# Last down projection of a hybrid encoder with its 512 tokens moved to the partitions: x turned by VectorE and transfers, final norm and output by groups of 128 tokens

## The chip, the cores and the metric

One core of a Trainium2 chip runs the whole program. The metric is the time of one execution on the device in microseconds (us); lower is better. TensorE (PE, with its weight loads PEld), VectorE (DVE), ScalarE (ACT), GpSimd (POOL) and the transfers (DMA, issued mostly by SyncE, SP) run beside each other, each engine its own instructions in order.

## The reference

Two layers on 512 tokens of width 1024 in float32. Each layer adds half a SwiGLU block, a mixer of attention and convolution, half a second SwiGLU block, and ends in an RMS norm:

```python
def swiglu(x, w_gate, w_up, w_down):
    return (jax.nn.silu(x @ w_gate) * (x @ w_up)) @ w_down
...
        x = x + 0.5 * swiglu(rms_norm(x, ffn2_norm[l]), ffn2_w_gate[l], ffn2_w_up[l], ffn2_w_down[l])
        x = rms_norm(x, post_norm[l])
    return x
```

`D_FF` is 2816. The change concerns the last `x @ w_down` of the second layer, the residual addition to it, and the last `rms_norm`.

## The kernel before

**Layout.** The residual `x` stays in on-chip memory as `[128, 8, 512]`: the 1024 features lie on the partitions in 8 blocks of 128, the 512 tokens along the free dimension. Every float32 product is made of three passes (`mm3`, lines 154 to 157): each operand is split into a high part (a cast on ScalarE, `hi`, `wh`) and a low part (a subtraction on VectorE, `lo`, `wl`), and high x high, high x low and low x high are added up in a bank of the accumulator memory. A weight tile of 128x1024 so costs one transfer, one cast of ScalarE (L240 or L144) and one subtraction of VectorE (L242 or L150).

**A SwiGLU block** (`ffn_body`) runs in units of up to four feature blocks of the 2816 (`UNITS = 2, 4, 4, 4, 4, 4`). The gate and up projections of a unit are made by a seven-product scheme on 2x2 blocks (`unit`), with sums of weight tiles made by VectorE (L338). The products are called by the operand that they use, in this order: `b11`, `b21`, `t2`, `t3`, `t1`, `t4`, `b22`, 24 matmuls each. They share banks: `t2` is added onto `bx`, `copied(bx)` (L354, on ScalarE) takes it away, and then `t1` is added onto the same two banks `bx`; `t3` and `t4` do the same on `bz`. So the first matmul of `t1` may only start when ScalarE has copied that bank.

The gated result of a unit has tokens on partitions and is turned for the down projection: VectorE transposes 32x32 blocks (L378), four transfers write a block to memory (`d<-e`, L384), two read it back as `r<-d` (L390), and `halved` (L396 on ScalarE, L397 on VectorE) splits it. A unit makes two such round trips through memory. Each unit's down projection is done while the next unit runs (`between`), so x is updated step by step (L486).

**The last stage** of a block takes the units that are left, the last two (8 feature blocks). Weights are stationary, activations `[128 features, 512 tokens]` are moved: for each of 8 output blocks, 8 x 3 matmuls of 128x512, then `update` adds the bank to `x[:, m, :]`, and `done(m)` does what the norm needs. In the last layer `done3` squares the block (ScalarE), adds it to a running sum (VectorE), and for the last block sums over the partitions by matmuls with a vector of ones (L193). Matmuls on ones (`idle`) fill TensorE's time there. After that comes `rsqrt` (a power on GpSimd, L173), `spread` (a diagonal matrix on VectorE, L207, and a matmul, L211, that puts the factor of each token into every partition), and eight products with gain and factor (L1018), each sent out as it is made (L1019).

**What sets the order.** The program is written in order, but a scheduler with its own estimate of durations decides how each engine's instructions stand; buffers come from pools that rotate: 4 each for `wh` and `wl`, 3 for `raw`, 9 for `fr` (the weight tiles of a unit), 7 banks called `ps`. A weight cast into `wh` waits until TensorE is through with the tile that lay in that buffer four tiles ago.

## Time and profile before

| | us |
|---|---|
| median of 3 runs | 1781.08 (1781.05 to 1782.27) |
| profiled execution, its own time | 1783.14 |
| its span | 1781.4 |
| TensorE's last matmul of the last stage starts | 1766.26 |
| mean granted TensorE clock | 0.996 |

| part of the span, us | VectorE busy | ScalarE busy | DMA share |
|---|---|---|---|
| 1680 to 1700 | 19.77 | 11.65 | 0.33 |
| 1720 to 1740 | 8.92 | 5.90 | 0.70 |
| 1740 to 1760 | 11.40 | 7.11 | 0.09 |

TensorE is busy for the whole of each of these stretches. In a timeline row, the first number is the start in us from the span's start, the second the time in us, then engine, line, operation, output and inputs, and in brackets how long the engine was idle before and for whom. A row with x2 or x8 merges instructions that follow each other.

### The profile page before, as it was taken

To read this page: it belongs to the slowest core of one execution; us is meant where nothing else is said; L and a number is where in the kernel's file an instruction comes from. 1 tells how busy PE (TensorE), PEld (TensorE's weight loads), DVE (VectorE), ACT (ScalarE), POOL (GpSimd) and SP (SyncE) were. 2 spreads that over 40 slices of the span, in tenths; PEclk is the share of its full clock that TensorE was granted. 3 is DMA by queue.
4 is the path that set the end of the run, shared out by engine and by line. 5 is a ranking of instruction groups with operands and counts; after the bars stand their busy time and mean duration, and the time that the engine had idled before them with its cause. 6 is when DMAs were issued, how large, how long until landed. Compare 5 with 4: busy or idle time off the path is not lost.

```text
span 1781.4 us, 22306 instructions
## 1 busy us (share of the span) xinstructions
PE 1756.3 (99%) x8208; PEld 1455.2 (82%) x8208; DVE 1403.5 (79%) x1984; ACT 946.4 (53%) x1472; POOL 277.7 (16%) x216
## 2 busy tenths in 40 slices
PE   8999999999999999999999999999999999999997
PEld 7788888888788888888888888888978788888886
DVE  7967877679869877878698778866979698678764
ACT  6544445457955544446555344444779455344442
POOL 4000000048842000000000000000688400000000
PEclk9999999999999999999999999999999999999999
DMA  8454434424225455343925344343250444345251
GB/s 287 138 165 143 146 110 126 135 77 130 49 104 133 128 158 164 109 152 94 290 78 170 114 154 142 113 125 115 80 152 3 159 115 163 131 142 161 88 154 60
DMA packets 119181, 234.09 MB, mean 131 GB/s; under 512 B 10272, under 2 KB 55712, under 8 KB 119072
## 3 DMA queue, kind: packets, MB, share of 16 engines
q1 hardware_dynamic: 115184, 219.72, 38.1%
q0 software_dynamic: 3456, 12.58, 3.9%
q8 instruction: 64, 1.05, 0.2%
q10 hardware_dynamic: 432, 0.38, 0.1%
q14 instruction: 45, 0.37, 0.1%
HBM read 207.47 MB, written 25.17 MB: 131 GB/s over the span
## 4 chain that ended last, share of the span: by engine, by line
PE 86%; DVE 4%; ACT 3%; DMA 3%; POOL 2%; issue 1%; SPq 1%; DVEq 0%; POOLq 0%; ACTq 0%
PE ps L157 27%; PE ps L155 27%; PE ps L156 27%; PE ps L796 2%; PE ps L762 1%; DVE wl L242 1%; DMA fr<-in_wgu 1%; DMA d<-e 1%; PE ps L783 1%; ACT pr L841 1%; PE ps L193 1%; POOL y L845 1%; ACT r L768 0%; DVE fr L338 0%; POOL sck L173 0%
## 5 line engine op out<-in xcount | busy, mean ns | idle before, releaser
L156 PE MATMUL ps<-wl,r 128*128 128x512 f32 (+2 forms) x1392 | 532.6, 384 | 1.6 <-DVE wl L242 1.4
L157 PE MATMUL ps<-wh,r 128*128 128x512 f32 (+2 forms) x1392 | 529.0, 384 | 2.7 <-DVE r L268 2.7
L155 PE MATMUL ps<-wh,r 128*128 128x512 f32 (+2 forms) x1392 | 514.2, 385 | 2.0 <-ACT wh L406 1.2
L240 ACT CAST wh<-fr 128x1024 fp32r<-128x1024 f32 x255 | 267.2, 1050 | 243.7 <-PE ps L156 113.4
L157 PE MATMUL ps<-r,wl 128*128 128x512 f32 x1008 | 391.0, 390 | 0.7 <-POOL wl L150 0.5
L156 PE MATMUL ps<-r,wh 128*128 128x512 f32 x1008 | 391.6, 390 | 0.0
L155 PE MATMUL ps<-r,wh 128*128 128x512 f32 x1008 | 386.8, 393 | 1.1 <-ACT r L396 0.7
L242 DVE TENSOR_TENSOR wl<-fr,wh 128x1024 fp32r<-128x1024 f32 x255 | 311.3, 1224 | 50.1 <-ACT wh L240 49.5
L157 PEld LDWEIGHTS ps<-wh,r 128*128 128x128 f32 x1392 | 261.8, 188 | 53.6 <-DVE r L268 3.6
L156 PEld LDWEIGHTS ps<-wl,r 128*128 128x128 f32 x1392 | 261.8, 188 | 53.3 <-DVE wl L242 3.3
L155 PEld LDWEIGHTS ps<-wh,r 128*128 128x128 f32 x1392 | 261.5, 188 | 53.1 <-ACT wh L406 1.4
L144 ACT CAST wh<-raw 128x1024 fp32r<-128x1024 f32 (+2 forms) x150 | 149.2, 1000 | 217.4 <-PE ps L156 95.0
L155 PEld LDWEIGHTS ps<-r,wh 128*128 128x128 f32 x1008 | 189.1, 188 | 43.6 <-ACT r L396 1.6
L157 PEld LDWEIGHTS ps<-r,wl 128*128 128x128 f32 x1008 | 189.3, 188 | 41.0 <-POOL wl L150 1.3
L156 PEld LDWEIGHTS ps<-r,wh 128*128 128x128 f32 x1008 | 189.3, 188 | 41.0 <-issue 1.4
L150 DVE TENSOR_TENSOR wl<-raw,wh 128x1024 fp32r<-128x1024 f32 (+3 forms) x134 | 157.2, 1175 | 70.5 <-ACT wh L144 69.2
L845 POOL TENSOR_TENSOR y<-y,pr 128x511 f32<-128x511 f32 (+14 forms) x120 | 157.9, 1316 | 56.3 <-ACT pr L841 49.5
L338 DVE TENSOR_TENSOR fr<-fr,fr 128x1024 f32<-128x1024 f32 x112 | 135.9, 1214 | 10.4 <-DMA fr<-in_wgu 10.4
L486 DVE TENSOR_TENSOR x<-ps,x 128x512 f32<-128x512 f32 x128 | 87.0, 685 | 71.9 <-PE ps L157 71.3
L173 POOL TENSOR_TENSOR rtok<-vtok,minus_half 128x4 f32<-128x4 f32 x8 | 10.4, 1303 | 743.6 <-DVE vtok L199 743.6
L368 ACT ACTIVATE e<-e,rtok 128x256 f32<-128x256 f32 x120 | 60.0, 508 | 83.9 <-DVE e L359 83.4
L397 DVE TENSOR_TENSOR r<-r,r 128x512 fp32r<-128x512 f32 x88 | 58.0, 679 | 56.2 <-ACT r L396 56.0
(175 smaller groups left out, 1732.1 us busy)
## 6 DMA issues: line engine op xcount, KB each, us to landing
fr<-in_wgu SPq DMA_DIRECT2D x175, 512.0 KB, 4.1
raw<-in_wd SPq DMA_DIRECT2D x64, 512.0 KB, 4.4
d<-e SPq DMA_DIRECT2D x176, 128.0 KB, 3.0
r<-d SPq DMA_DIRECT2D x88, 256.0 KB, 3.6
raw<-in_wd SPq DMA_DIRECT2D x32, 384.0 KB, 4.4
raw<-in_wcv SPq DMA_DIRECT2D x16, 512.0 KB, 3.2
raw<-in_wout SPq DMA_DIRECT2D x16, 512.0 KB, 3.7
raw<-in_wgu SPq DMA_DIRECT2D x8, 512.0 KB, 4.6
```

Of the source, the lines that this page charges most:

```text
L144: A.copy(hi[:, :w], raw[:, :w])
L150: (G if kind in POOLW.split() else V).tensor_tensor(lo[:, :w], raw[:, :w], hi[:, :w].bitcast(FP), ALU.subtract)
L155: T.matmul(o, lh, rh, start=first, stop=False, skip_group_check=free)
L156: T.matmul(o, lh, rl, start=False, stop=False, skip_group_check=free)
L157: T.matmul(o, ll, rh, start=False, stop=last, skip_group_check=free)
L240: order["cast"] = A.copy(hi[:, :w], src[:, :w]).ins
L242: V.tensor_tensor(lo[:, :w], src[:, :w], hi[:, :w].bitcast(FP), ALU.subtract)
L338: V.tensor_tensor(oh, ah, bh, ALU.add)
L368: A.activation(out[j][:, :h], src[j][:, :h], AF.Silu, scale=r)
L397: V.tensor_tensor(d, d.bitcast(FP), hi.bitcast(FP), ALU.subtract)
L486: V.tensor_tensor(xm, pd.rearrange("p (a t j) -> p t a j", a=4, t=NT), xm, ALU.add)
L845: order["conv"] = G.tensor_tensor(acc[:, s:], acc[:, s:], pr[:, s:], ALU.add).ins
```

## The change

In the last SwiGLU block of the last layer (`done is None`) the last stage is replaced by `end`:

- **x is turned.** VectorE transposes x in 32 instructions of 128x128 (four tiles `tb`, one for each block of 128 tokens, L521), and 16 transfers of 128 KB (32 partitions x 4 x 256 numbers, L528) put the pieces back into the memory of `x`, which then holds, as `xt`, 4 groups of 128 tokens on the partitions with 1024 features each. Both can be done as soon as the unit before has updated x, so they stand in the last unit.
- **The products are turned.** Activations are stationary (128 tokens of a feature block), weights `wend` `[128, 1024]` are moved in halves of 512: 8 accumulators (7 banks `ps` and one called `cv`), 4 groups x 2 halves. The first four feature blocks go through all accumulators; the last four finish one accumulator after the other. The weight tiles have the same size and number as before.
- **The norm goes by groups.** For each half: addition to `xt`, square with a sum along the free dimension on ScalarE. For each group: two small steps on VectorE, the power on GpSimd for one column, then one half of the output by VectorE and one by ScalarE, and two transfers of 256 KB. The post norm's gain is loaded once as `[128, 1024]` (`gend`) and is multiplied into the first half ahead of the factor.
- The host reorders the weights and the output for the block order that 32x32 transposes give.

```diff
+        ending = done is None
...
+        def weights(i):
+            raw = wpool.tile([P, WC], FP, tag="raw", name=nm("raw"), bufs=3)
+            nc.sync.dma_start(out=raw, in_=wend[i])
+            if i < 6:
+                return split_into("q", raw)
+            hi, lo = (fpool.tile([P, WC], FR, tag="fr", name=nm("fr"), bufs=FRB) for _ in range(2))
+            A.copy(hi, raw)
+            V.tensor_tensor(lo, raw, hi.bitcast(FP), ALU.subtract)
+            return hi, lo
+
+        def end(acts, ds):
+
+            n = len(ds)
+            tb = [fresh() for _ in range(NT)]
+            for m in range(KD):
+                for t in range(NT):
+                    V.transpose(tb[t].rearrange("p (a m j) -> p a m j", a=4, m=KD)[:, :, m],
+                                x[:, m, t * P:(t + 1) * P])
+            gb = fresh()
+            nc.sync.dma_start(out=gb, in_=gend)
+            xt = x.rearrange("p (a h) s -> p a (h s)", a=4)
+            for t in range(NT):
+                for b in range(4):
+                    nc.sync.dma_start(
+                        out=xt[t * 32:(t + 1) * 32, :, b * HS:(b + 1) * HS],
+                        in_=tb[t][b * 32:(b + 1) * 32].rearrange("p (a f) -> p a f", a=4))
+            os = [[bank() for _ in range(2)] for _ in range(3)]
+            os.append([bank(), psum.tile([P, S], FP, tag="cv", name=nm("cv"), bufs=1)])
...
+            for i in range(n):
+                w = weights(i)
+                for a in range(4):
+                    for h in range(2):
+                        part(os[a][h], acts[i], w, a, h, i == 0, False)
+            acts.extend(halved(d) for d in ds)
+            ws = [weights(i) for i in range(n, 2 * n)]
+            ss, ve = tiny("ssend", 8), tiny("veend", 4)
+            for a in range(4):
+                for h in range(2):
+                    f = slice(h * S, (h + 1) * S)
+                    for i in range(n):
+                        part(os[a][h], acts[n + i], ws[i], a, h, False, i == n - 1)
+                    V.tensor_tensor(xt[:, a, f], xt[:, a, f], os[a][h], ALU.add)
+                    A.activation(tmp(), xt[:, a, f], AF.Square, accum_out=ss[:, 2 * a + h:2 * a + h + 1])
+                    if h == 0:
+                        V.tensor_scalar(ve[:, a:a + 1], ss[:, 2 * a:2 * a + 1], 1.0 / D, EPS, ALU.mult, ALU.add)
+                        V.tensor_tensor(xt[:, a, f], xt[:, a, f], gb[:, f], ALU.mult)
+                V.scalar_tensor_tensor(ve[:, a:a + 1], ss[:, 2 * a + 1:2 * a + 2], 1.0 / D, ve[:, a:a + 1],
+                                       ALU.mult, ALU.add)
+                r = tiny("rend", 1)
+                rsqrt(r, ve[:, a:a + 1])
+                o = [slot(), slot()]
+                V.scalar_tensor_tensor(o[1], xt[:, a, S:WC], r, gb[:, S:WC], ALU.mult, ALU.mult)
+                nc.sync.dma_start(out=out[a, :, S:WC], in_=o[1])
+                A.activation(o[0], xt[:, a, 0:S], AF.Copy, scale=r)
+                (A if a == 3 else nc.sync).dma_start(out=out[a, :, 0:S], in_=o[0])
...
+        if ending:
+            return end(acts, ds)
...
-            ffn(l, ops, norm2, wgu2, wd2, done3)
-            r = tiny("rlast", NT)
-            rsqrt(r, ve)
-            ps = spread(r)
-            for m in range(KD):
-                o = slot()
-                V.scalar_tensor_tensor(o, x[:, m, :], gp[:, m:m + 1], ps, ALU.mult, ALU.mult)
-                nc.sync.dma_start(out=out[m], in_=o)
+            ffn(l, ops, norm2, wgu2, wd2, None)
```

Up to the last unit of this block the order of the instructions stays what it was, but for line numbers (one more from L320 on). In the last unit the scheduler places things anew. Three places follow; the number behind a name tells one buffer from the next, and the two programs number them apart by one.

**VectorE, start of the last unit**, before: `e_14217` is a gate result on its way to the first round trip, `e_14361` the block that this round trip will carry, `wl_14521` and `wl_14525` the low parts of the first weight tiles.

```order
L359 TENSOR_TENSOR e_14217<-ps_14254,e_14217 128x512
L242 TENSOR_TENSOR wl_14521<-fr_14499,wh_14519 128x1024
L359 TENSOR_TENSOR e_14217<-ps_14255,e_14217 128x512
L369 SCALAR_TENSOR_TENSOR e_14217<-e_14217,rh_12685 128x256
L338 TENSOR_TENSOR fr_14499<-fr_14499,fr_14507 128x1024
L242 TENSOR_TENSOR wl_14525<-fr_14501,wh_14523 128x1024
L378 STREAM_TRANSPOSE e_14361<-e_14217 128x8x32
```

The same place now:

```order
L360 TENSOR_TENSOR e_14216<-ps_14253,e_14216 128x512
L521 STREAM_TRANSPOSE fr_14826<-x 128x4x32 x8
L242 TENSOR_TENSOR wl_14520<-fr_14498,wh_14518 128x1024
L360 TENSOR_TENSOR e_14216<-ps_14254,e_14216 128x512
L370 SCALAR_TENSOR_TENSOR e_14216<-e_14216,rh_12684 128x256
L242 TENSOR_TENSOR wl_14524<-fr_14500,wh_14522 128x1024
L339 TENSOR_TENSOR fr_14498<-fr_14498,fr_14506 128x1024
L379 STREAM_TRANSPOSE e_14360<-e_14216 128x8x32
```

The first eight transposes of x stand ahead of the first weight tile's low part and of all that follows. Up to this block's last transpose, six rows further on, one gate product (L370 on `t_14482`) has moved ahead of it too.

**VectorE, around the weights of `t3`** (`wl_14654` and `wl_14658` before, `wl_14653` and `wl_14657` now), before:

```order
L242 TENSOR_TENSOR wl_14621<-fr_14501,wh_14619 128x1024
L242 TENSOR_TENSOR wl_14654<-raw_14515,wh_14652 128x1024
L359 TENSOR_TENSOR e_14551<-e_14551,ps_14566 128x512
L359 TENSOR_TENSOR e_14551<-e_14551,ps_14567 128x512
L397 TENSOR_TENSOR r_14447<-r_14447,r_14554 128x512
L397 TENSOR_TENSOR r_14449<-r_14449,r_14557 128x512
L242 TENSOR_TENSOR wl_14658<-raw_14516,wh_14656 128x1024
```

The same place now:

```order
L242 TENSOR_TENSOR wl_14620<-fr_14500,wh_14618 128x1024
L521 STREAM_TRANSPOSE fr_14827<-x 128x4x32 x8
L242 TENSOR_TENSOR wl_14653<-raw_14514,wh_14651 128x1024
L360 TENSOR_TENSOR e_14550<-e_14550,ps_14565 128x512
L360 TENSOR_TENSOR e_14550<-e_14550,ps_14566 128x512
L521 STREAM_TRANSPOSE fr_14828<-x 128x4x32 x7
L242 TENSOR_TENSOR wl_14657<-raw_14515,wh_14655 128x1024
L521 STREAM_TRANSPOSE fr_14828<-x 128x4x32
L398 TENSOR_TENSOR r_14446<-r_14446,r_14553 128x512
L398 TENSOR_TENSOR r_14448<-r_14448,r_14556 128x512
```

Fifteen more transposes stand ahead of the second of them, and the two low halves of the first round trip (L398) have gone behind it. The last eight transposes follow a few rows later.

**ScalarE, between `t2` and `t1`**, before: `r_14560` and `r_14563` are the casts of the second round trip, `wh_14689` to `wh_14730` weight casts, `e_14647` the copies of `bx`, two banks.

```order
L396 CAST r_14560<-r_14495 128x512
L368 ACTIVATE e_14551<-e_14551,rtok_12683 128x256
L396 CAST r_14563<-r_14497 128x512
L240 CAST wh_14689<-fr_14507 128x1024
L354 COPY e_14647<-ps_14517 128x512
L354 COPY e_14647<-ps_14518 128x512
L240 CAST wh_14693<-fr_14509 128x1024
L240 CAST wh_14730<-fr_14511 128x1024
```

The same place now:

```order
L240 CAST wh_14688<-fr_14506 128x1024
L397 CAST r_14559<-r_14494 128x512
L397 CAST r_14562<-r_14496 128x512
L369 ACTIVATE e_14550<-e_14550,rtok_12682 128x256 x2
L240 CAST wh_14692<-fr_14508 128x1024
L240 CAST wh_14729<-fr_14510 128x1024
L240 CAST wh_14733<-fr_14512 128x1024
L355 COPY e_14646<-ps_14516 128x512
L355 COPY e_14646<-ps_14517 128x512
```

The copies of `bx` have moved behind three weight casts, `wh_14692`, `wh_14729` and `wh_14733`; the last of these takes the buffer of `wh_14655`, the second weight tile of `t3`.

More of the change, by code (lines that the diff above doesn't have):

```diff
@@ L73, in encoder_kernel @@
 def encoder_kernel(ctx: ExitStack, tc: tile.TileContext, xT, consts, vecs, rgain, wgu1, wd1,
[L74 removed]
+                   wcv, wql, wkl, wuq, wkv, wout, wgu2, wd2, wend, gend, out):
     nc = tc.nc
@@ L502, in down2, with part @@
                 update(m0 + i, pd)
+        def weights(i):
[24 more added lines that the diff above has]
+            os.append([bank(), psum.tile([P, S], FP, tag="cv", name=nm("cv"), bufs=1)])
+            def part(o, act, w, a, h, first, last):
+                c, f = slice(a * P, (a + 1) * P), slice(h * S, (h + 1) * S)
+                mm3(o, act[0][:, c], act[1][:, c], w[0][:, f], w[1][:, f], first, last, True)
+            for i in range(n):
[25 more added lines that the diff above has]
+                (A if a == 3 else nc.sync).dma_start(out=out[a, :, 0:S], in_=o[0])
@@ L1065 @@
     turns = turns.reshape(F)
+    wend = a["ffn2_w_down"][L - 1][turns][(NF - 8) * P:]
+    wend = wend.reshape(8, P, KD, 4, 32).transpose(0, 1, 3, 2, 4).reshape(8, P, D)
+    gend = a["post_norm"][L - 1].reshape(KD, 4, 32).transpose(1, 0, 2).reshape(1, D)
     vec = np.zeros((P, L, VN), f32)
@@ L1108 @@
     r = run_bass_kernel_spmd(nc, [arrays], core_ids=[0])
-    got = np.asarray(r.results[0]["out_T"]).reshape(D, S)
-    return np.ascontiguousarray(got.T)[None]
+    got = np.asarray(r.results[0]["out_T"]).reshape(4, NT, 32, 4, KD, 32)
+    return np.ascontiguousarray(got.transpose(1, 0, 2, 4, 3, 5).reshape(S, D))[None]
```

15 lines of the change are left out of this document (2 added, 13 removed).

## The prediction

> **What bounds the kernel now.** I read the page first, then the busy time by stretches, then the timeline of the last 60 us engine by engine.
>
> ```profile
> span 1781.4 us, 22306 instructions
> PE 1756.3 (99%) x8208; PEld 1455.2 (82%) x8208; DVE 1403.5 (79%) x1984; ACT 946.4 (53%) x1472; POOL 277.7 (16%) x216
> ```
>
> ```profile
> 1680.00:1700.00 20.00, 20.00 (x90) 16.58 (x89) 19.77 (x26) 11.65 (x16) 0.00 (x0) 1.00 0.33 82
> ...
> 1767.00:1781.40 14.40, 5.42 (x38) 4.30 (x38) 6.75 (x12) 0.63 (x1) 1.01 (x1) 0.80 0.39 146
> ```
>
> The columns of the second fence are the stretch and its length, then busy us (with instructions) of PE, PEld, DVE, ACT and POOL, the granted clock, the DMA share and GB/s. TensorE never rests until the last product is done; only what lengthens its row of matmuls or what follows it costs time. Two places matter. In 1680 to 1700, the last unit's first half, VectorE is busy 19.77 of 20 us: it has nothing to spare just where the change puts work. And from 1767 on nothing is left to TensorE but a tail, which is this chain:
>
> ```profile
> 1766.26 0.39 PE L157 MATMUL ps<-r,wl 128*128 128x512 f32 x1
> ...
> 1766.69 0.69 DVE L486 TENSOR_TENSOR x<-ps,x 128x512 f32<-128x512 f32 x1 [3.30 <-PE ps L157]
> ...
> 1767.47 0.63 ACT L1009 ACTIVATE t<-x 128x512 f32<-128x512 f32 x1 [4.81 <-DVE x L486]
> ...
> 1768.16 1.05 PE L193 MATMUL ps<-ones,t 128*128 128x1 f32 x8
> ...
> 1769.25 0.16 DVE L1010 SCALAR_TENSOR_TENSOR vlast<-ps,vlast 128x4 f32<-128x4 f32 x1 [1.61 <-PE ps L193]
> 1769.49 1.01 POOL L173 TENSOR_TENSOR rlast<-vlast,minus_half 128x4 f32<-128x4 f32 x1 [311.77 <-DVE vlast L1010]
> 1770.53 0.69 DVE L207 TENSOR_TENSOR t<-cst,rlast 128x512 f32<-128x512 f32 x1 [1.12 <-POOL rlast L173]
> ...
> 1771.37 1.10 PE L211 MATMUL ps<-t,ones 128*128 128x512 f32 x2
> 1772.51 5.36 DVE L1018 SCALAR_TENSOR_TENSOR r<-x,vec,ps 128x512 f32<-128x512 f32 x8 [1.28 <-PE ps L211]
> 1773.28 4.94 SPq L1019 DMA_DIRECT2D out_T<-r  x8
> ```
>
> The last matmul ends at 1766.26 + 0.39 = 1766.65, the span at 1781.4: a tail of 14.75 us. The last output tile is made at 1772.51 + 5.36 = 1777.87; its transfer and the end take the other 3.53.
>
> **The matmuls** stay the same in number: 8 blocks of 24 before, 8 accumulators with 24 each after, all 128x512.
>
> ```profile
> 1722.97 0.39 PE L155 MATMUL ps<-r,wh 128*128 128x512 f32 x1
> ```
>
> This is the first of those 192 and 1766.26 the last, so one follows another every 43.29 / 191 = 0.2267 us. If nothing makes TensorE wait, it is done at 1766.65 again.
>
> **The new tail**, counted from T, the end of the last matmul. Two prices are new and come from other places:
>
> ```profile
> L173 POOL TENSOR_TENSOR rtok<-vtok,minus_half x8: 1021/1038/1932, 35.1 to 1456.7; 128x4 f32<-128x4 f32 x8
> L173 POOL TENSOR_TENSOR scq<-ssh,minus_half x8: 1635/1647/4757, 411.2 to 1303.8; 128x8 f32<-128x8 f32 x8
> ```
>
> ```profile
> L608 ACT ACTIVATION_READ_ACCUMULATOR t<-ps x8: 201/240/280, 400.7 to 1281.6; 128x1 f32 x8
> ```
>
> The addition starts at T + 0.04 (1766.69 after 1766.65) and the square 0.78 later (1767.47 after 1766.69), at T + 0.82. The square's sum comes out by an accumulator read: 0.52 until it starts, 0.24 for itself, T + 1.58. VectorE's small step starts at T + 1.62, GpSimd 0.24 after it (1769.49 after 1769.25). GpSimd's power on one column isn't in the trace. Four columns take 1.02, eight 1.64, so the line through both gives 0.56; 1.02 is the upper end. I take 0.56: T + 2.42. The last product with the gain, 0.69 on VectorE, ends at T + 3.15, with ScalarE's half beside it. With 3.53 for transfer and end, the tail is **6.7 us** instead of 14.75: 8.05 saved. What goes is the sum over partitions on TensorE, the spreading of the factor (L207, L211) and seven of the eight output products. What is late next is the order on VectorE: the addition of the last half stands behind the gain product of its neighbour, and this behind the factor of group 2. By the same steps with 0.56 VectorE gets free at T - 0.12, so it costs nothing; with 1.02 it costs 0.3, and the tail is 7.5.
>
> **What is put ahead of it.** 32 transposes of 128x128 go into VectorE's row in the last unit, 8 + 8 + 7 + 1 + 8.
>
> ```profile
> 1679.19 0.68 DVE L359 TENSOR_TENSOR e<-ps,e 128x512 f32<-128x512 f32 x1
> 1679.79 1.21 DVE L242 TENSOR_TENSOR wl<-fr,wh 128x1024 fp32r<-128x1024 f32 x1
> ...
> 1686.44 1.22 DVE L242 TENSOR_TENSOR wl<-fr,wh 128x1024 fp32r<-128x1024 f32 x1
> 1687.58 0.44 DVE L378 STREAM_TRANSPOSE e<-e 128x256 f32<-128x256 f32 x1
> 1687.94 0.40 DVE L378 STREAM_TRANSPOSE e<-t 128x256 f32<-128x256 f32 x1
> ...
> 1690.89 0.44 DVE L378 STREAM_TRANSPOSE e<-t 128x256 f32<-128x256 f32 x1
> ...
> 1698.16 1.22 DVE L242 TENSOR_TENSOR wl<-raw,wh 128x1024 fp32r<-128x1024 f32 x1
> ```
>
> From start to start 1024 elements take 1.14, 512 take 0.60: 1.055 ns an element. A 256-wide transpose takes 0.36, of which 0.27 are elements and 0.09 fixed; a 128-wide one then takes 0.135 + 0.09 = 0.225. Bounds: 0.19 (the fixed part of the wider operations, 0.06) and 0.36 (as dear as the 256-wide). I take 0.225, being the same operation.
>
> The Trainium skill, VectorE: DVE Perf Modes, section on the TRN2 errata, speaks against this edit: the latency of SBUF is exposed once per instruction, so many small tiles pay it many times, and tiles of 512 elements or more are advised. The trace agrees (0.09 fixed in 0.36). The page's table on the three transpose paths has 311 ns for a 128x128 block; at that the stall below would be 2.9 instead of 2.2 and the forecast 1775.9, an estimate from that page.
>
> First check, VectorE's own lateness. The split that started at 1698.16 (second weight tile of `t3`) is the tightest: 23 transposes stand ahead of it (5.2 us), two low halves of 0.6 now come behind it, so it ends near 1703.4. TensorE needs it 82 matmuls before 1722.97, at 1704.38. One us is left: no stall at 0.225, one of 2.2 at 0.36.
>
> Second check, and here I find **a new wait**. In the last unit ScalarE's `copied(bx)` before `t1` has moved behind three weight casts, and `t1` adds onto that same bank, so its first matmul waits for the copy.
>
> ```profile
> 1688.04 1.85 SPq L384 DMA_DIRECT2D d<-e  x4
> 1691.86 0.81 SPq L390 DMA_DIRECT2D r<-d  x2
> 1692.77 1.97 SPq L384 DMA_DIRECT2D d<-e  x4
> 1698.56 0.81 SPq L390 DMA_DIRECT2D r<-d  x2
> ```
>
> ```profile
> 1701.33 0.62 ACT L396 CAST r<-r 128x512 fp32r<-128x512 f32 x1 [3.49 <-DMA r<-d]
> 1701.85 0.51 ACT L368 ACTIVATE e<-e,rtok 128x256 f32<-128x256 f32 x1
> 1702.27 0.60 ACT L396 CAST r<-r 128x512 fp32r<-128x512 f32 x1
> 1702.78 1.05 ACT L240 CAST wh<-fr 128x1024 fp32r<-128x1024 f32 x1
> 1703.72 1.06 ACT L354 COPY e<-ps 128x512 f32<-128x512 f32 x2
> 1704.68 2.00 ACT L240 CAST wh<-fr 128x1024 fp32r<-128x1024 f32 x2
> ```
>
> Before, the first copy was done at about 1704.3; `t1` starts 72 matmuls ahead of 1722.97, at 1706.65, so 2.3 us were to spare. After: the block's last transpose (1687.58 before) has eight new transposes (1.80) and one more gate product (0.36) ahead of it, so the round trip through memory starts 2.16 later, at 1690.2, and the second block's follows it on SP's queue as before. (That block's last transpose starts two 0.36 and three 1.14 steps after 1689.74 and ends at 1694.3; SP wants it at 1692.77 + 2.16 = 1694.9.) ScalarE gets its operand at 1701.33 + 2.16 = 1703.49. Then come two casts (0.52 and 0.51), two activations (0.42 each), three weight casts (0.95 each), the copy (0.59) and 0.05 to TensorE: 1708.85. The stall is **2.2 us**. There is a floor that no speed on VectorE removes: the third cast writes a buffer that the last matmul of `t3` reads, which ends at 1706.81; 0.05 + 0.95 + 0.59 + 0.05 later is 1708.45, a stall of 1.8. At 0.36 a transpose, `t3` itself ends 2.2 late and the floor becomes 4.0. At 0.19 the stall is 1.9. I take 2.2.
>
> **The rest is covered.** The 16 transfers that bring the x blocks home (128 KB each, like `d<-e`, 0.46 to issue) and the gain's load wait for VectorE's last eight transposes, near 1712 by the same prices, and leave SP's queue by 1718, ahead of the last unit's own round trips:
>
> ```profile
> 1722.50 2.38 SPq L384 DMA_DIRECT2D d<-e  x4
> ```
>
> ```profile
> 1731.91 1.28 ACT L396 CAST r<-r 128x512 fp32r<-128x512 f32 x2 [7.32 <-DMA r<-d]
> 1736.76 1.27 ACT L396 CAST r<-r 128x512 fp32r<-128x512 f32 x2 [3.57 <-DMA r<-d]
> ```
>
> The first `d<-e` comes 2 to 3 later, with TensorE's products that it carries; with a weight load more between the steps I put the operands some 4 us later, and with their casts and the last weights ready at 1744. Before, TensorE had 48 matmuls of other work to cover this wait, now 96: it asks at 1722.97 + 2.2 + 21.8 = 1747. If that 3 us cover were gone, each us beyond it would cost one.
>
> **Sum**, against the profiled execution: -14.75 + 6.7 + 2.2 = -5.85. Its span 1781.4 becomes 1775.55. That execution took 1783.14; the median of the runs is 1781.08, and the same difference gives **1775.2**.
>
> **Rivals.**
> - *No stall* (7%): ScalarE reaches the copy in time. 1781.08 - 8.05 = 1773.0. For it: 2.3 us were spare. Against it: the floor of 1.8.
> - *Dear transposes* (13%): 0.36 each, VectorE becomes the bound, stall 4.0, time 1777.0. For it: 19.77 of 20 us busy. Against it: the smaller element count.
> - *Slower than before* (4%): the same place, but the write in four strided pieces of 32 makes a transpose far dearer. The stall is 23 x (price - 0.225) + 0.9 (1.0 to spare, then the 1.8 of the cast and the copy); it eats the 8.05 from 0.54 us a transpose, and at 0.7 us gives 1784.8. Against it: the 256-wide one writes strided pieces of 32 already, in 0.36.
> - *The tail doesn't shrink as said* (8%): the factor of group 2, ScalarE's half and the last additions queue up on each other, each with a GpSimd step, and 3 us come back: 1778.2.
> - *Late operands* (8%): the 2 MB of x transfers hold up the `d<-e` round trip by 6 us instead of being done before; 3 beyond the cover, 1778.2.
> - *Forecast* (60%): stall 1.8 to 2.9, tail 6.2 to 7.5.
>
> The **range** reaches from the first rival's 1773.0 to 1778.0, short of the two cases at 1778.2 and the slower one (20%). About 0.2% (3.6 us) is what a measurement of this kernel can tell from no change, so faster means below 1777.5: 80%; the same 16%; slower 4%.
>
> **What would show it.** Right: TensorE's wait list names ScalarE's copy (L355) once, about 2 us, and nothing else after 1640; transposes at L521 follow each other every 0.22 to 0.23; the last matmul ends near 1768.9; GpSimd takes 0.5 to 0.7 for one column; the span ends 6.7 after the last matmul. Wrong: TensorE waits for VectorE's `wl` (transposes too dear), for `r` or `wh` in the last stage (late operands), or a tail above 8 us.

## The result, and the profile after

The changed kernel takes 1777.78 us (median of 18 runs, 1774.26 to 1782.9) beside 1781.67 for the kernel before, timed with it (18 runs, 1779.84 to 1784.66). The ratio is 0.9976 with a 95% interval of 0.997 to 0.9983: faster by 0.24%, or 4.3 us (3.9 between the medians), where 5.85 were forecast. The prediction drew its line for faster at 1777.5, 3.6 below 1781.08, the median of its three runs; 1777.78 is above that line, but more than 3.6 below the kernel before as timed beside it.

The first fence is the head of the profile page of the changed kernel, the second its busy time by stretches (columns as in the prediction).

```profile
span 1776.1 us, 22289 instructions
PE 1750.7 (99%) x8166; PEld 1448.9 (82%) x8166; DVE 1406.0 (79%) x2015; ACT 951.8 (54%) x1484; POOL 279.1 (16%) x219
```

```profile
1680.00:1700.00 20.00, 20.00 (x90) 16.55 (x89) 20.00 (x38) 11.66 (x15) 0.00 (x0) 1.00 0.34 80
...
1769.00:1776.10 7.10, 0.00 (x0) 0.00 (x0) 1.60 (x3) 1.45 (x3) 0.54 (x1) 0.68 0.20 74
```

VectorE's last 0.23 us of slack in 1680 to 1700 are gone, and the stretch behind the last product is 7.1 us long instead of 14.4.

Single spans are a poor measure here. Until the last unit the queues of all the kernels below hold the same instructions on every engine (but for the source of one weight load), and still they reach it at times that lie 5 us apart (1677.97 to 1683.26). So each profile is read from a **common row**, the pair of matmuls near 1680.7 that stands at the same place of the program in every trace. Counted so, the changed kernel and the two variants that differ from it only behind the last matmul (e_pow4, e_pieces) agree within 0.01: 87.87 to the start of the last matmul in all three. Before, then after:

```profile
1680.81 0.61 PE L155 MATMUL ps<-wh,r 128*128 128x512 f32 x2
```

```profile
1680.70 0.61 PE L155 MATMUL ps<-wh,r 128*128 128x512 f32 x2
...
1706.31 0.39 PE L157 MATMUL ps<-wh,r 128*128 128x512 f32 x1
1708.32 0.50 PE L155 MATMUL ps<-wh,r 128*128 128x512 f32 x1 [1.62 <-ACT e L355]
1708.66 0.39 PE L156 MATMUL ps<-wl,r 128*128 128x512 f32 x1
...
1747.67 0.39 PE L157 MATMUL ps<-wh,r 128*128 128x512 f32 x1
1747.90 0.40 PE L155 MATMUL ps<-fr,r 128*128 128x512 f32 x1
...
1768.57 0.39 PE L157 MATMUL cv<-fr,r 128*128 128x512 f32 x1
```

From the common row to the start of the last matmul it was 1766.26 - 1680.81 = 85.45; now it is 1768.57 - 1680.70 = 87.87, so 2.42 were lost on the way. Two places show them. From 1706.31 to 1708.66 there should be two steps of 0.2267, and there are 2.35: the wait at L355 costs **1.90**. From 1747.90 to 1768.57 the 89 steps take 20.67, which is 0.2322 a step instead of 0.2267: **0.50** that nothing in the prediction had. (The 0.02 that are left lie right behind the wait, where five steps to 1709.82 take 0.232.) The tail after the last matmul went from 14.75 to 1776.1 - 1768.96 = 7.14: **7.61** saved. From the common row to the end the change is -7.61 + 2.42 = **-5.19** (95.40 after 100.59).

For matmuls, TensorE's list of waits after 1650 has one entry (who waited, for whom, us in total, times, longest; a second one gives the weight load at the same place 2.0):

```profile
PE ps L155 <- ACT e L355: 1.6, 1, 1.6
```

What ScalarE, the engine waited for, did ahead of it:

```profile
1702.61 0.62 ACT L397 CAST r<-r 128x512 fp32r<-128x512 f32 x1 [2.72 <-DMA r<-d]
1703.43 0.62 ACT L397 CAST r<-r 128x512 fp32r<-128x512 f32 x1 [0.21 <-DMA r<-d]
1703.96 0.91 ACT L369 ACTIVATE e<-e,rtok 128x256 f32<-128x256 f32 x2
1704.77 3.01 ACT L240 CAST wh<-fr 128x1024 fp32r<-128x1024 f32 x3
1707.69 2.05 ACT L355 COPY e<-ps 128x512 f32<-128x512 f32 x4
```

It idled for 2.72 until the late operand came home, and then took two casts, two activations and three weight casts ahead of the copy, one after another.

VectorE's transposes, and the split that the prediction's first check named (1700.89, the second weight tile of `t3`):

```profile
1679.26 1.65 DVE L521 STREAM_TRANSPOSE fr<-x 128x128 f32<-128x128 f32 x8
...
1699.51 1.46 DVE L521 STREAM_TRANSPOSE fr<-x 128x128 f32<-128x128 f32 x7
1700.89 1.18 DVE L242 TENSOR_TENSOR wl<-raw,wh 128x1024 fp32r<-128x1024 f32 x1
1701.99 0.30 DVE L521 STREAM_TRANSPOSE fr<-x 128x128 f32<-128x128 f32 x1
```

Eight from 1679.26 to the next instruction at 1680.83: 0.196 each.

And the tail, put together from the timelines of VectorE, ScalarE and GpSimd:

```profile
1769.00 0.69 DVE L551 TENSOR_TENSOR x<-x,cv 128x512 f32<-128x512 f32 x1 [0.27 <-PE cv L157]
1769.78 0.63 ACT L552 ACTIVATE t<-x 128x512 f32<-128x512 f32 x1 [1.83 <-DVE x L551]
1770.32 0.18 ACT L552 ACTIVATION_READ_ACCUMULATOR t<-x 128x1 f32 x1
1770.77 0.54 POOL L173 TENSOR_TENSOR rend<-veend,minus_half 128x1 f32<-128x1 f32 x1 [5.03 <-DVE veend L556]
1771.35 0.75 DVE L561 SCALAR_TENSOR_TENSOR r<-x,rend,fr 128x512 f32<-128x512 f32 x1 [0.66 <-POOL rend L173]
1772.10 0.39 ACTq L564 DMA_DIRECT2D out_T<-r  x1
```

With T = 1768.96, the last product ends at 1772.10, T + 3.14; transfer and end take 4.00 more.

### The profile page after: what moved, and what is told of

The parts are those of the page before. It is cut to its first block, busy times and chain, and to the rows that moved or that the text cites. A ratio compares the mean times of both kernels' runs of the same rounds, so it can differ in the third digit from the quotient of the medians.

```text
span 1776.1 us, 22289 instructions
## 1 busy us (share of the span) xinstructions
PE 1750.7 (99%) x8166; PEld 1448.9 (82%) x8166; DVE 1406.0 (79%) x2015; ACT 951.8 (54%) x1484; POOL 279.1 (16%) x219
## 4 chain that ended last, share of the span: by engine, by line
PE 86%; DVE 4%; DMA 3%; ACT 3%; issue 1%; POOL 1%; SPq 1%; POOLq 0%; ACTq 0%; DVEq 0%
PE ps L157 27%; PE ps L155 27%; PE ps L156 27%; PE ps L860 2%; DMA fr<-in_wgu 1%; DVE wl L242 1%; PE ps L826 1%; PE ps L847 1%; DMA d<-e 1%; ACT r L832 1%; DVE fr L339 1%; ACT pr L905 1%; PE ps L193 0%; DMA r<-d 0%; POOL sck L173 0%
## 5 line engine op out<-in xcount | busy, mean ns | idle before, releaser
L156 PE MATMUL ps<-wl,r 128*128 128x512 f32 (+2 forms) x1434 | 549.0, 384 | 1.6 <-DVE wl L242 1.4
L157 PE MATMUL ps<-wh,r 128*128 128x512 f32 (+2 forms) x1434 | 545.4, 384 | 1.3 <-DVE r L268 1.3
L155 PE MATMUL ps<-wh,r 128*128 128x512 f32 (+2 forms) x1434 | 530.4, 385 | 2.9 <-ACT e L355 1.6
L157 PE MATMUL ps<-r,wl 128*128 128x512 f32 x944 | 365.9, 390 | 1.0 <-DVE wl L150 0.5
L156 PE MATMUL ps<-r,wh 128*128 128x512 f32 x944 | 366.5, 390 | 0.2 <-DVE r L398 0.2
L155 PE MATMUL ps<-r,wh 128*128 128x512 f32 x944 | 362.4, 393 | 1.9 <-ACT r L397 1.2
L155 PEld LDWEIGHTS ps<-wh,r 128*128 128x128 f32 x1434 | 269.5, 188 | 55.5 <-ACT e L355 2.0
L156 PEld LDWEIGHTS ps<-wl,r 128*128 128x128 f32 x1434 | 269.7, 188 | 54.8 <-DVE wl L242 2.7
L157 PEld LDWEIGHTS ps<-wh,r 128*128 128x128 f32 x1434 | 269.5, 188 | 53.9 <-DVE r L268 2.1
L144 ACT CAST wh<-raw 128x1024 fp32r<-128x1024 f32 (+2 forms) x142 | 140.6, 994 | 212.8 <-PE ps L156 85.5
L155 PEld LDWEIGHTS ps<-r,wh 128*128 128x128 f32 x944 | 177.0, 188 | 42.2 <-ACT r L397 2.7
L156 PEld LDWEIGHTS ps<-r,wh 128*128 128x128 f32 x944 | 177.2, 188 | 39.0 <-issue 1.4
L157 PEld LDWEIGHTS ps<-r,wl 128*128 128x128 f32 x944 | 177.2, 188 | 38.9 <-POOL wl L150 1.3
L150 DVE TENSOR_TENSOR wl<-raw,wh 128x1024 fp32r<-128x1024 f32 (+3 forms) x126 | 147.5, 1172 | 73.6 <-ACT wh L144 73.0
L398 DVE TENSOR_TENSOR r<-r,r 128x512 fp32r<-128x512 f32 x88 | 57.8, 678 | 45.3 <-ACT r L397 45.1
```

What stands on the lines that cost most here:

```text
L144: A.copy(hi[:, :w], raw[:, :w])
L150: (G if kind in POOLW.split() else V).tensor_tensor(lo[:, :w], raw[:, :w], hi[:, :w].bitcast(FP), ALU.subtract)
L155: T.matmul(o, lh, rh, start=first, stop=False, skip_group_check=free)
L156: T.matmul(o, lh, rl, start=False, stop=False, skip_group_check=free)
L157: T.matmul(o, ll, rh, start=False, stop=last, skip_group_check=free)
L398: V.tensor_tensor(d, d.bitcast(FP), hi.bitcast(FP), ALU.subtract)
```

## The experiments

**Theory**: the transposes are covered, and the stall is the place of `copied(bx)` in ScalarE's queue, behind casts that wait for a round trip and for a weight buffer. **Rival**: VectorE is full in the last unit, and the copy is only where it shows. A second question is the step of 0.2322. All numbers are us: from the common row to the start of the last matmul, the tail from its end to the end of the span, and the sum, from the common row to the end of the span (with the last matmul's own 0.39 or 0.40). Spans are printed to 0.1, so tail and sum are good to 0.05. The waits are those of the list for matmuls, which counts idle time; the steps can show more. Each row is one trace.

| kernel | to last matmul | tail | sum | TensorE waits (list) |
|---|---|---|---|---|
| before | 85.45 | 14.75 | 100.59 | none ahead of the tail |
| changed | 87.87 | 7.14 | 95.40 | 1.6 at L355 |
| e_copy | 86.58 | 7.14 | 94.11 | 0.3 for `wl` |
| e_late | 85.80 | 7.58 | 93.78 | none |
| e_noturn | 85.96 | 7.23 | 93.58 | none |
| e_twice | 91.20 | 7.24 | 98.83 | 3.4 at L355 |
| e_best_twice | 88.68 | 7.19 | 96.26 | 2.6 for `wl` |
| e_ktile | 87.68 | 11.10 | 99.18 | 1.6 at L355 |
| e_swapfr | 88.12 | 7.25 | 95.76 | 1.8 at L355 |
| e_ring | 87.37 | 7.13 | 94.89 | 1.6 at L355 |
| e_wide | 87.88 | 7.20 | 95.47 | 1.6 at L355 |
| e_best | 85.68 | 7.17 | 93.24 | none (0.3 for `wl` in weight loads) |

### e_copy: the copy ahead of the casts

```diff
+            hold = lambda i: tc.issue_after(order[i]) if ending and u == last else nullcontext()
+            order["c"] = order["copy"]
...
-            product(bx, a21, "t1", False, True)
+            product(bx, a21, "t1", False, True, hold)
+            if ending and u == last:
+                with hold("cast"):
+                    d = sides(copied(bz, N))
+                    acts.extend(halved(v) for v in ds[2:])
...
+            with hold("copy"):
+                product(bz, a22, "t4", False, True)
```

> In the last unit ScalarE takes t2's copy ahead of t1's second weight cast, of t4's two casts and of the casts of the late operand pair; the transposes stay where they are. Theory (the stall is the place of the copy in ScalarE's queue): TensorE's wait for L355's copy (1.78 us in the changed kernel) is gone; at most 0.4 us comes back as a wait for the low half of t1's second weight tile; the last matmul ends 1.4 to 1.8 us earlier and the span is 1774.3 to 1774.7 where that of the changed kernel was 1776.1. Rival (VectorE, 10 of 10 us busy, is what limits the last unit, and the copy is only where it shows): the wait moves to a low half from VectorE and at least 1.2 us of it stay; span 1775.5 to 1776.1.

The edit also moves the casts of the late operands, and `t4`'s, behind the copy; the transposes stay. ScalarE's timeline now has the copy where it was idle before:

```profile
1700.59 1.05 ACT L372 ACTIVATE e<-e,rtok 128x256 f32<-128x256 f32 x2
1701.55 1.06 ACT L358 COPY e<-ps 128x512 f32<-128x512 f32 x2
1702.49 1.06 ACT L240 CAST wh<-fr 128x1024 fp32r<-128x1024 f32 x1
```

The wait for the copy is gone, and the last matmul comes 1.29 earlier. That is a little less than the theory's 1.4 to 1.8, and far from the rival's "at least 1.2 stay". The rest is the small wait that was foreseen, larger than foreseen: from 1709.35 TensorE loses 0.60 (its list says 0.3) because VectorE made eight of the new transposes (and two others) ahead of the low half of `t1`'s second weight tile:

```profile
1706.83 1.26 DVE L532 STREAM_TRANSPOSE fr<-x 128x128 f32<-128x128 f32 x6
...
1708.35 0.46 DVE L532 STREAM_TRANSPOSE fr<-x 128x128 f32<-128x128 f32 x2
...
1709.06 1.18 DVE L242 TENSOR_TENSOR wl<-fr,wh 128x1024 fp32r<-128x1024 f32 x1
```

In time: 1774.52 us (5 runs), ratio to before 0.9958 (0.9944 to 0.9971).

### e_late and e_noturn: the turn later, or left out

```diff
+            order["c"] = order["turn"]
...
-            for m in range(KD):
-                for t in range(NT):
+            with tc.issue_after(order["c"]):
+                for m in range(KD):
+                    for t in range(NT):
```

> The 32 transposes are held back behind the last unit's second turn, so VectorE's row in its first half is that of the kernel before; the 16 transfers home then start near 1729 instead of 1701. Theory: no wait for L355's copy, because with VectorE's operands 2 us earlier ScalarE reaches the copy ahead of the casts; the transposes themselves, 32 x 0.195 = 6.2 us, are covered between 1722 and 1730. The price can only be late operands: the last weight loads stand behind the 16 transfers on SP's queue (16 x 0.46 = 7.4 us), so TensorE may wait 0 to 3 us for a weight near 1746. Span 1774.3 without that wait, up to 1777 with it. Rival (the turn costs by itself, wherever it stands): a wait of about 2 us for VectorE's low halves or for x appears after 1722.

No wait is left, and the last matmul starts 85.80 after the common row. The scheduler again has the copy (1703.53) ahead of two of the three casts, so this run alone can't tell the copy's place from VectorE's lighter load. The late operands cost nothing either: the last three weight casts came at 1747.52, 1749.41 and 1750.78, and the scheduler had put the matmuls that need them behind those of the other tiles. The tail is 0.44 longer: on VectorE the last addition now stands behind its neighbour's gain product and starts 0.38 after the last matmul instead of 0.04.

e_noturn drops the 32 transposes and the 16 transfers, so its output isn't that of the block.

```diff
-            tb = [fresh() for _ in range(NT)]
-            for m in range(KD):
-                for t in range(NT):
-                    V.transpose(tb[t].rearrange("p (a m j) -> p a m j", a=4, m=KD)[:, :, m],
...
-            for t in range(NT):
-                for b in range(4):
-                    nc.sync.dma_start(
```

> Leaves out the turning of x: no transposes at L521 and no transfers home, so the residual that is added in the last stage is x as it lies. Theory: the turn costs the 1.78 us at L355 and nothing else; without it ScalarE reaches the copy in time, the last matmul starts 86.1 us after the row at 1680.7 (85.45 and 0.64 for the fr tiles), the tail is 7.1 and the span 1774.3. Rival (the transposes or the 2 MB of transfers slow something else as well): more than 2 us are gained.

Without the turn the scheduler itself puts the copy ahead of two of the three casts, and TensorE waits for nothing:

```profile
1704.47 1.06 ACT L355 COPY e<-ps 128x512 f32<-128x512 f32 x2
1705.42 2.01 ACT L240 CAST wh<-fr 128x1024 fp32r<-128x1024 f32 x2
```

The last matmul comes 87.87 - 85.96 = 1.91 earlier, which is the 1.90 of the stall and nothing more. With the 0.50 of the slow steps taken off, 85.46 is left, the 85.45 of the kernel before. So neither the transposes nor the 2 MB of transfers cost anything beside the stall.

### e_twice and e_best_twice: how much cover there is

```diff
+                    for _ in range(2):
...
                         V.transpose(tb[t].rearrange("p (a m j) -> p a m j", a=4, m=KD)[:, :, m],
```

> Each of the 32 transposes is made twice, with the same result: 32 x 0.195 = 6.2 us more on VectorE. Theory: VectorE's rows in the last unit have slack that the placing of the work finds; the wait at L355 stays at 1.8 to 2.3, any other wait is below 0.5, span 1776.1 to 1777. Rival (VectorE is the bound of the last unit, as in the case of dear transposes): the second weight tile of t3 or t1 comes late and TensorE waits at least 2.8 us more (23 x 0.195 less the 1.7 that were to spare at 0.195), span 1778.9 or more.

Here my theory gave the wrong number, and the rival the wrong place. The last matmul comes 3.33 later than in the changed kernel, but no weight tile is late: it is the copy again, now 3.4. Only 1.77 of the 3.33 are the longer wait (two steps take 4.12 there instead of 2.35); the other 1.56 were lost right behind it, where the granted clock fell to 0.50 (1713 to 1715) and a step took 0.427. So the rival's "at least 2.8" was reached with the help of a clock that it didn't have in its sum. ScalarE shows why the copy is late.

```profile
1704.22 0.51 ACT L369 ACTIVATE e<-e,rtok 128x256 f32<-128x256 f32 x1
1707.96 1.32 ACT L397 CAST r<-r 128x512 fp32r<-128x512 f32 x2 [3.23 <-DMA r<-d]
1709.18 1.04 ACT L240 CAST wh<-fr 128x1024 fp32r<-128x1024 f32 x1
1710.13 2.04 ACT L355 COPY e<-ps 128x512 f32<-128x512 f32 x4
```

Only one weight cast stands ahead of the copy, but so do the casts of the late operands, and their round trip starts when VectorE has made the block's last transpose. More work on VectorE makes the round trip later, and the queue hands this on to a copy that has nothing to do with it. So the two theories are not apart: here VectorE sets how late the copy is, and ScalarE's order lets that reach TensorE. To take the order out, e_best (below) got the doubled turn as well.

> e_best with each transpose made twice (6.2 us more on VectorE). It asks whether the wait of e_twice (3.4 us at L355) was ScalarE's queue alone. If it was, the wait goes with the copy's place and TensorE waits less than 0.5 in all; the last matmul starts 85.5 to 86 after the row at 1680.7. If VectorE's row is full by itself once the turn is doubled, TensorE waits for the low halves of t1's second and t4's first weight tile, 2 to 5 us together, and the last matmul starts at 87.5 to 90.5. After e_twice I hold the second to be likelier.

The second case came: no wait at L355, and 2.6 us for two low halves from VectorE, which is busy for all of 1710 to 1715 (who waited, for whom, us in total, times, longest).

```profile
PE ps L156 <- DVE wl L242: 2.6, 2, 1.7
```

The last matmul starts at 88.68. So 32 transposes are covered (to within 0.2, as e_best shows) and 64 are not, with or without the copy in the way.

### e_ktile, e_swapfr, e_ring, e_wide: the step of 0.2322

e_ktile changes the loops of the second half:

```diff
+            for i in range(n):
+                for a in range(4):
+                    for h in range(2):
+                        part(os[a][h], acts[n + i], ws[i], a, h, False, i == n - 1)
...
-                    for i in range(n):
-                        part(os[a][h], acts[n + i], ws[i], a, h, False, i == n - 1)
```

> The second half of the last stage goes weight tile by weight tile over the eight accumulators, as the first half does, instead of finishing one accumulator after another. It asks why the matmul pitch is 0.232 us from 1747.9 on instead of 0.2267. If it is the twelve matmuls in a row into one bank, the pitch is 0.2267 throughout and the last matmul ends 0.6 earlier. If it is the weight tiles of L510 (buffers named fr), the matmuls of the first two weight tiles keep 0.2267 and those of the last two show 0.23 to 0.235. The tail gets longer in either case: the last 12 matmuls before the end (2.7 us) finish four accumulators, so additions (0.60 each) and squares (0.63 + 0.2 each) of several groups stand behind one another; I expect a tail of 10 to 12 us instead of 7.1 and a span of 1779 to 1781.

The steps are 0.2267 through the second half's first two tiles and change with the first matmul on `fr` (three steps later TensorE is 0.71 on, not 0.68):

```profile
1756.21 0.39 PE L157 MATMUL cv<-wh,r 128*128 128x512 f32 x1
1756.43 0.40 PE L155 MATMUL ps<-fr,r 128*128 128x512 f32 x1
...
1757.14 0.40 PE L155 MATMUL ps<-fr,r 128*128 128x512 f32 x1
```

From 1756.43 the 47 steps to 1767.40 take 0.2334 each. So it isn't the order of the accumulators. The tail is 11.10, as expected from four groups that end together.

e_swapfr changes which tiles go to `fr`:

```diff
-            if i < 6:
+            if i not in (4, 5):
```

> The weight tiles that go into the fr buffers are the fifth and sixth of the last stage instead of the seventh and eighth; nothing else is meant to move. If the fr buffers make the pitch, the slow matmuls (0.2345 a piece in the changed kernel, against 0.230 for those between them) are now those of the fifth and sixth tile. If it is the operands of the seventh and eighth (late r tiles), they stay with these whatever buffer the weights lie in. If it is the order of accumulators, the pitch stays 0.232 over all. Span 1776.1 within 0.3 in each case.

The slow steps went with the buffers: three matmuls on `fr` (now the fifth and sixth tile) take 0.70, three on `wh` and `wl` 0.69. The last matmul is 0.25 later than in the changed kernel, because this trace's stall is 0.2 longer: its late operand came 0.41 later, counted from the common row (1702.16 - 1679.84 = 22.32 beside 1702.61 - 1680.70 = 21.91).

e_ring puts them into `r` slots (`part` then takes the half that it needs):

```diff
-            hi, lo = (fpool.tile([P, WC], FR, tag="fr", name=nm("fr"), bufs=FRB) for _ in range(2))
...
+            pieces = [split(raw[:, h * S:(h + 1) * S]) for h in range(2)]
+            return [p[0] for p in pieces], [p[1] for p in pieces]
```

> Only the last two weight tiles of the last stage are moved: into r slots (the ring at 33 to 118 KB of a partition) instead of fr buffers (174 to 207 KB). If the place of the moving operand sets the pitch, all matmuls are at 0.2267 again and the last one starts 87.2 us after the row at 1680.7 instead of 87.87; L355's wait of 1.6 to 1.8 stays. If the slow ones are slow for another reason (their left operands, their age), tiles seven and eight keep 0.233 wherever they lie. Span 1775.4 or 1776.1.

With the tiles in `r` slots every step is 0.2267 again, and the last matmul comes 0.50 earlier (87.37), the whole of what was to explain; three steps are 0.68:

```profile
1761.61 0.39 PE L155 MATMUL ps<-r,r 128*128 128x512 f32 x1
...
1762.29 0.39 PE L155 MATMUL ps<-r,r 128*128 128x512 f32 x1
```

e_wide puts them into `e` buffers:

```diff
-            hi, lo = (fpool.tile([P, WC], FR, tag="fr", name=nm("fr"), bufs=FRB) for _ in range(2))
+            hi, lo = (fpool.tile([P, WC], FR, tag="e", name=nm("e"), bufs=WIDE) for _ in range(2))
```

> Only the last two weight tiles of the last stage are moved once more: into buffers of the e tiles, which this kernel has at 208 to 228 KB of a partition, above the fr buffers (171 to 208 KB); the wh and wl tiles lie at 119 to 152 KB, the r slots below. If a high place makes the moving operand slow, tiles seven and eight keep 0.233 or more, and the last matmul starts 87.8 to 88 after the row at 1680.7. If it is something of the fr buffers alone, all matmuls are at 0.2267 and the last one starts at 87.35, as in e_ring. Nothing else should move: L355's wait of 1.6 stays.

The `e` buffers are as slow as `fr` (87.88; three steps are 0.71):

```profile
1760.36 0.40 PE L155 MATMUL ps<-e,r 128*128 128x512 f32 x1
...
1761.07 0.40 PE L155 MATMUL ps<-e,r 128*128 128x512 f32 x1
```

So in the last stage the step follows the place of the moving operand: 0.2267 where it lies below 152 KB of a partition, 0.2334 (e_ktile) in the two groups of buffers above 171 KB. The places are those of the program's buffers; no trace shows an address (the ring begins at 23 and ends at 105 KB, not 33 and 118 as the expectation of e_ring has it, still below 152). Where between them it changes, and why the `wh` matmuls among the slow ones take 0.230, stays open. Slow steps are also not a matter of place alone: behind the wait at L355 five steps with `wh` and `wl` take 0.232 (1708.66 to 1709.82), and then 0.2267 again.

### e_pow4 and e_pieces: the tail

```diff
-                r = tiny("rend", 1)
-                rsqrt(r, ve[:, a:a + 1])
+                r = tiny("rend", 4 if a == 3 else 1)
+                rsqrt(r, ve if a == 3 else ve[:, a:a + 1])
```

> On the changed kernel: GpSimd's power for the last group is taken on four columns instead of one (the same factor is used). It prices the width alone. By the line through four and eight columns the step takes 1.02 instead of 0.54, and the last product ends 3.62 after the last matmul instead of 3.14; span 0.48 longer beyond the common row. Rival (GpSimd's price is fixed and 0.54 was a chance): no change in the tail.

```profile
1768.87 1.02 POOL L173 TENSOR_TENSOR rend<-veend,minus_half 128x4 f32<-128x4 f32 x1 [5.02 <-DVE veend L556]
```

GpSimd takes 1.02, and the last product ends 1770.68 - 1767.06 = 3.62 after the last matmul, both as the theory had them; the tail is 7.74.

```diff
+                for c in [slice(0, S)] if a < 3 else [slice(0, HS), slice(HS, S)]:
...
+                    nc.sync.dma_start(out=out[a, :, d], in_=o[1][:, c])
...
+                    (nc.sync if a < 3 else A if c.start else G).dma_start(out=out[a, :, c], in_=o[0][:, c])
```

> On the changed kernel: the last group's two output halves are made and sent in four pieces of 256 columns, the first two pieces 0.35 us ahead of the others. The changed kernel's last two transfers of 256 KB leave at one time and land 2.3 and 2.7 us after their issue, where those of the kernel before left 0.6 apart and took 2.1. If they share the DMA engines, the pieces end the tail 0.2 to 0.4 earlier (6.75 to 6.95 instead of 7.14). If the price is per transfer, nothing is gained, or 0.1 to 0.3 lost.

The tail is 7.27, 0.13 longer: the rival. The list of transfers (KB each, us from issue to landing) shows that half the size saves little:

```profile
out_T<-r SPq DMA_DIRECT2D x2, 256.0 KB, 2.2
out_T<-r SPq DMA_DIRECT2D x2, 128.0 KB, 2.1
out_T<-r POOLq DMA_DIRECT2D x1, 128.0 KB, 2.8
out_T<-r ACTq DMA_DIRECT2D x1, 128.0 KB, 2.0
```

### e_best: what the experiments point to

It joins e_copy and e_ring and holds the last eight transposes behind the low half that e_copy waited for:

```diff
+            order["t1"] = order["low"]
...
+                    with tc.issue_after(order["t1"]) if t == 3 else nullcontext():
```

> Three edits on the changed kernel: ScalarE takes t2's copy ahead of the weight casts (as in e_copy), the last eight transposes stand behind the low half of t1's second weight tile (so that e_copy's rest of 0.3 goes too), and the last two weight tiles are split into four 512-wide r slots instead of two fr buffers. Theory: nothing waits on TensorE after 1640, the pitch is 0.2267 to the end, and the last matmul starts 85.4 to 85.6 us after the row at 1680.7 (85.45 in the kernel before, 87.87 in the changed one); tail 7.1; span 1773.6 to 1773.9 beside 1776.1, time 2.2 to 2.5 below the changed kernel's. Rival (the waits only move on): a wait of 0.5 us or more for a low half from VectorE or for a late operand takes their place, and the time is e_copy's or worse.

No matmul stands in the list of waits, every step of the last stage is 0.2267, and the last matmul starts 85.68 after the common row. Of the 0.23 too many, 0.17 lie in the two steps from 1714.77, where a weight load is named:

```profile
PEld ps L156 <- DVE wl L242: 0.3, 1, 0.3
```

This low half is that of `t4`'s first weight tile, and the eight transposes that were held back stand ahead of it now: for 0.17 us the wait did move on, as the rival said. The sum is 2.16 below the changed kernel's. The profiled execution reached the common row late (1683.26), so its span, 1776.5, misses the expected 1773.6 to 1773.9 all the same. The time is 1773.95 us (5 runs, 1773.07 to 1778.27), ratio to before 0.9956 (0.9942 to 0.997). It beats the kernel before. The changed kernel's ratio, 0.997 to 0.9983 beside its own runs of before, only touches this one at 0.997; against e_copy the times can't tell it apart. The common row tells it from both (93.24 beside 95.40 and 94.11), by one trace of each.

## Why the prediction came out as it did

- **The tail** was right step by step: the last product ends at T + 3.14 (forecast 3.15), GpSimd's single column takes 0.54 (0.56, from the line through four and eight columns, which e_pow4 confirms). What was too small is "transfer and end 3.53", taken from a row of eight transfers 0.6 apart: it is 4.00. Both last transfers now leave at one time (1772.10 and 1772.13). ScalarE's lands 2.7 us after its issue, the median of SyncE's five is 2.3, and before it was 2.1; tail 7.14 instead of 6.7.
- **The new wait** was right in place and cause: the copy at L355 behind three weight casts, once. Its cost is 1.90, between the floor of 1.8 and the 2.2 taken. The operand came 0.9 earlier than forecast (its cast started at 1702.61, not 1703.49), and the round trip began at 1689.44, not 1690.2. Cheaper transposes are only 0.23 of that (eight at 0.196 instead of 0.225). 0.11 is this trace's earlier common row, and 0.42 is luck: counted from that row, VectorE came to the new transposes earlier than the trace of before came to the same place (1679.26 - 1680.70 beside 1679.79 - 1680.81). Then the floor is what is left: the third cast starts near 1706.7, when the last matmul of `t3` frees its buffer. The traces of e_pieces and e_swapfr show the floor. In e_pieces the operand's cast starts 1699.44 - 1677.97 = 21.47 after the common row (21.91 in the changed kernel), and the third cast still starts at 26.04, as in the changed kernel, because it now waits for TensorE:

```profile
1704.01 1.05 ACT L240 CAST wh<-fr 128x1024 fp32r<-128x1024 f32 x1 [0.59 <-PE ps L157]
```

  The wait at L355 is 1.6 in both. In e_swapfr, with the operand at 22.32, ScalarE's row is what is late, and the wait is 1.8. So the floor sets the cost here, and an operand only 0.2 later (an estimate: 0.41 later cost 0.2) would have handed it back to ScalarE's row.
- **The transposes** were mis-sized on the safe side: 0.196 each for 0.225, near the lower bound of 0.19. The first check's split ended at 1702.07, 2.2 ahead of its need (ten steps before 1706.54, where `t1` would have started) instead of 1.0. The Trainium skill's 311 ns for a 128x128 block (VectorE: DVE Perf Modes, section on the three transpose paths) is near the length of one record here, 0.27 to 0.30, but they overlap, and a sum needs the distance between them. So the estimate of 1775.9 by that page rested on the wrong one of two durations. The Trainium skill's advice against small tiles (same page, section on the TRN2 errata) cost nothing to ignore here: e_noturn shows that the turn had no price beside the stall.
- **The matmuls** were the step that failed: "one follows another every 0.2267", taken from the stage before, where every moving operand lies lower. Two of the eight weight tiles went to `fr` buffers, and 0.50 us went with them. The line of the diff that puts them there (L510) has no part in the prediction's sum.
- **Late operands** were covered as said; no wait for them in any kernel.
- **The sum**: -8.05 + 2.2 = -5.85 was forecast and -7.61 + 1.90 + 0.50 = -5.19 came (by 0.02 of rounding). The interval of the ratio, 3.0 to 5.3 us, holds the second and not the first. So 0.66 of the 2.6 us between 1775.2 and 1777.78 are explained. Of the rest, 0.6 is the kernel before itself (1781.67 beside the 1781.08 that was taken); where the other 1.3 lie isn't shown. They may lie before the common row, which the traces reach up to 5 us apart.
- **Luck.** The time lies 0.22 inside the upper end of a range 5 us wide. And the last matmul ended at 1768.96, where 1768.9 was forecast, only because errors cancelled: the slow steps that were missing (+0.50) against a stall taken 0.3 too long and a trace that began the last unit 0.1 earlier.

Of the rivals, "no stall" fell to the floor that spoke against it, "dear transposes" and "slower than before" to the 0.196, the longer tail to 7.14, and "late operands" to a list without such a wait. What e_twice adds is that the mechanism of "dear transposes" was real and only its place was wrong: with twice the work VectorE does delay TensorE, first through the round trip and ScalarE's queue.

## What to carry to other kernels

When work goes into a gap of one engine, look at the queue of the engine that feeds from it: there a step that needs nothing of the new work can stand behind one that does. Moving one copy ahead of some casts was worth 1.3 us on top of 5.2. And in this kernel a matmul's step went with the place of its moving operand as well as with its shape, so a tile that is put into other buffers needs its own row, or a place like that of the others.

## What the hardware showed beside this

- In the last stage the step of a 128x512 fp32r matmul went with the moving operand's place: 0.2267 below 152 KB of a partition, 0.2334 in the buffers above 171 KB, 3% more.
- After e_twice's wait of 3.4 us the clock was halved for a while; after the 1.6 of the changed kernel it was not. The stretches right behind the wait, e_twice first (the figure after POOL is the granted clock):

```profile
1711.00:1716.00 5.00, 5.00 (x16) 3.92 (x16) 5.00 (x14) 2.53 (x5) 0.00 (x0) 0.66 0.24 96
```

```profile
1708.30:1713.30 5.00, 4.98 (x22) 4.13 (x23) 4.52 (x13) 2.49 (x4) 0.00 (x0) 1.00 0.96 241
```

  The Trainium skill, TensorE: Matmul & The Clock Gate, section on HAM oscillation, advises against idle gaps of TensorE above about 3.4 us; these two waits fit it, but shorter ones don't keep the clock safe here. The same wait of 2.04 us for ScalarE (L762 before, L826 now) was followed by 0.66 over 5 us in the trace of before (from 1333.80) and by 1.00 in that of the changed kernel (from 1332.10), and one of 1.44 us by 0.66 in e_twice (from 46.20) and 1.00 in the changed kernel (from 46.60). A mean of 0.66 over 5 us is 1.7 us, an estimate; in e_twice the steps show 1.56 lost on top of the wait.
- GpSimd's power costs by the column: 0.54, 1.02 and 1.64 us for one, four and eight.
- A transfer of 128 KB lands hardly sooner than one of 256 KB (2.0 to 2.1 and 2.1 to 2.3 us; 2.7 for one on ScalarE's queue), and on GpSimd's queue later (2.8).
